# A single-core encoder block in split single precision: the rotary key's projection, the rotation, the small latent scores and the order of the first head pair are changed

## The chip, the cores and the metric

One core of a Trainium2 chip runs the whole program. Its engines are TensorE (PE: matrix products; PEld is its loading of the stationary operand), VectorE (DVE), ScalarE (ACT), GpSimd (POOL) and the DMA queues, of which this kernel uses nearly only the one that SyncE (SP) issues. Each engine carries out its own list of instructions in order; semaphores hold an instruction until what it needs is done. The metric is the device time of one execution in microseconds, smaller is better. A profiled execution gives the span from the first to the last instruction, and what each engine did in it.

## The reference, cut to what matters

272 tokens (256 real ones and 16 meta tokens) of width 2048 pass through one layer: neighbourhood attention (8 heads, "NA") and latent attention (8 heads, "MLA") side by side, an output projection, and a gated MLP. The change lies in the latent attention, where a key has 128 plain dimensions of its own head and 64 rotary ones that all heads share:

```python
def apply_rope(x, cos, sin):
    x1, x2 = x[..., :half], x[..., half:]
    return jnp.concatenate([x1 * cos - x2 * sin, x2 * cos + x1 * sin], axis=-1)
...
    q = (rmsnorm(cq, cq_g) @ w_q_up).reshape(B, L, MLA_HEADS, MLA_QK_DIM)
    kv = (rmsnorm(ckv, ckv_g) @ w_kv_up).reshape(B, L, MLA_HEADS, MLA_NOPE_DIM + MLA_V_DIM)
    k = jnp.concatenate([k_nope, jnp.broadcast_to(k_pe[:, :, None, :], (B, L, MLA_HEADS, MLA_ROPE_DIM))], axis=-1)
    q, k = rmsnorm(q, q_g), rmsnorm(k, k_g)
    q = jnp.concatenate([q[..., :MLA_NOPE_DIM], apply_rope(q[..., MLA_NOPE_DIM:], cos, sin)], axis=-1)
    k = jnp.concatenate([k[..., :MLA_NOPE_DIM], apply_rope(k[..., MLA_NOPE_DIM:], cos, sin)], axis=-1)
    s = jnp.einsum('bqhd,bkhd->bhqk', qb, k).astype(jnp.float32) * scale
```

`cq` (512 columns), `ckv` (256) and `k_pe` (64) are projections of the normed input `hn`, as are the queries, keys and values of the neighbourhood heads.

## The kernel before

**Products.** Every operand is held as a rounded part and a remainder (hi and lo). A product is then three matmuls, w_hi x_hi, w_hi x_lo and w_lo x_hi (`mm3`, lines 485 to 487, and `product3`, line 842). Tokens are the moving columns, 258 where only the queries are wanted (256 and two copied meta columns) or 272.

**Weights.** They come in pieces of up to 1024 columns (`pieces`, line 335 on). SP loads a piece into one of five `raw` buffers, ACT copies it to a `whi` buffer (four, line 450), DVE subtracts to make `wlo` (four, line 459), PE uses each 128 columns. A `raw` buffer is loaded again when its subtraction is done, a `whi`/`wlo` pair is written again when PE has used it.

**Order.** There is no scheduler on the chip for this. The program is written as threads (`Flow`, line 100), and while the kernel is built a planner with a price for each instruction decides which thread's next instruction is appended to which engine's list. What stands in the lists is then fixed; an engine that reaches an instruction too early waits, and all behind it with it.

**Stages of PE.** `attention_weights` (line 1391): projection to `cq` (64 blocks of three matmuls), to `ckv` (32), to the rotary key (16; its 64 columns stand twice in the 128 of a block), then for each of four head pairs the stages of `ORDER = "QKqkVv"`: Q, K, V are the up-projections of the latent heads (from `cq` and `ckv`), q, k, v the projections of the neighbourhood heads (from the input). Scores, softmax and products with V of one stage are laid between the projections of later ones. Then come the output projection and the MLP, which the change leaves alone.

**The steps that change.** `sum_x` (line 601) adds the squares of 16 input tiles on DVE into `sqx`; `scale_x` (line 656) sums them over partitions by a matmul with ones and makes the scales `em1` and `s1`. `compressed_kv` (line 711) normalizes `ckv`, which stage K needs. `rotary_key` (line 746) scales the projected key. `rope` (line 737) rotates: a single-precision matmul with the constant matrix `rot` swaps the halves (line 740), POOL multiplies by cos, DVE multiplies the swapped half by sin out of PSUM, POOL adds. It runs once for the key (272 columns) and once for each pair's two queries (258). `mla_rope` (line 1125) splits the rotated query into `mqr`; `mla_tile` (line 1213) uses it with both parts of the key `mkp`. `mla_small` (line 1239) makes the scores of the copied meta queries, four stationary columns `qs` for two heads: five matmuls of 272 columns for each head, ten for each pair.

Of the kernel before, what the change touches and what calls it, by code (L numbers as in the profile page):

```python
# [15 lines left out]
P = 128  # L16
# [39 lines left out]
ORDER = "QKqkVv"  # L56
# [3 lines left out]
CW = 32  # L60
KP = 2 * CW + N_META
# [14 lines left out]
CONSTS = {"ident": 0, "ones": 128, "rot": 256, "cos": 384, "sin": 384 + L}  # L76
N_CONSTS = 384 + 2 * L
# [117 lines left out]
def encoder_block(ctx: ExitStack, tc: tile.TileContext, io):  # L195
# [104 lines left out]
    class Piece:  # L300
# [6 lines left out]

        def release(self):
            fl.put(raws, self.raw)

# [36 lines left out]
    for i in range(3):  # L347
        add(io["w_in"][i])
    n_in = 3
    for pr in range(4):  # L350
        for stage in ORDER:
# [91 lines left out]
    def split_hi():  # L443
        for p in pieces:
            yield p.loaded
            p.hi = yield from one(his)
            for t, ev in zip(p.parts, p.half):
                if p is pieces[0]:
                    yield p.part[t.start]
                yield from ACT(p.hi[:, t], p.raw[:, t], AF.Copy)  # L450
                fl.set(ev)
            n_split[0] += 1

    def split_lo():
        for p in pieces:
            p.lo = yield from one(los)
            for t, ev, ready in zip(p.parts, p.half, p.ready):
                yield ev
                yield from TT(p.lo[:, t], p.raw[:, t], p.hi[:, t].bitcast(F32), ALU.subtract)
# [251 lines left out]
    def compressed_kv(pss):  # L711
        t0, t1, a, b, r = yield scr, 5
        ts = (t0, t1)
        for i, ps in enumerate(pss):
            yield from ACT(ts[i][:, :L], ps[:, :L], AF.Copy, scale=vec("g_ckv", i))
            yield from ACT((a, b)[i][:, :L], ps[:, :L], AF.Square)
            fl.put(tps, ps)
# [7 lines left out]
        for i, t in enumerate(ts):  # L725
            yield from TT(t[:, :L], t[:, :L], r[:, :L], ALU.mult)
            yield from ACT(ckv[i][0], t[:, :L], AF.Copy)
            yield from TT(ckv[i][1], t[:, :L], ckv[i][0].bitcast(F32), ALU.subtract)
            fl.put(scr, t)
        for t in (a, b, r):  # L730
            fl.put(scr, t)
        fl.set(ev_ckv)

# [3 lines left out]
    def rope(t, n, out, tmp):  # L737

        r = yield from one(sps)
        yield from MM([(r[:, :n], const("rot"), t, True, True)])  # L740
        yield from PTT(out, t, const("cos", n), ALU.mult)
        yield from TT(tmp[:, :n], r[:, :n], const("sin", n), ALU.mult)
        fl.put(sps, r)
        yield from PTT(out, out, tmp[:, :n], ALU.add)

    def rotary_key(ps):
        yield ev_s1
        t, kg, tmp = yield scr, 3
        yield from TT(t[:, :L], ps[:, :L], s1, ALU.mult)
        fl.put(acc, ps)  # L750
# [33 lines left out]
    qss = tiles(apool, 2, [P, 36], "qs", F32R)  # L784
# [104 lines left out]
    def small_queries(s):  # L889
# [3 lines left out]
        t = s.qs[:, :24].rearrange("p (l c x) -> p l c x", l=2, c=2)  # L893
        for i in range(2):
            yield "pool", 150
            nc.gpsimd.tensor_copy(t[:, i, :, 0:2], s.q[:, :, i, SEQ:NT])
        fl.set(s.ev_small)

# [145 lines left out]
    def na_small(s, pr, PT, done):  # L1044
# [7 lines left out]
        for c in range(2):  # L1052
            q = [s.qs[:, 12 * i + 4 * c : 12 * i + 4 * c + 4] for i in range(2)]
# [55 lines left out]
    mqr = Slots(tiles(apool, 1, [P, 2, NT], "mqr", F32R))  # L1109
    mk = Slots(late[6:])  # L1110
    mkp = Slots(tiles(apool, 2, [P, 2, L], "mkp", F32R))
# [13 lines left out]
    def mla_rope(s, g, t, tmp):  # L1125
# [4 lines left out]
        for c in range(2):  # L1130
            e, o = slice(64 * c, 64 * c + 64), slice(64 - 64 * c, 128 - 64 * c)
            yield from ACT(s.qr[e, c, :], t[e, :NT], AF.Copy)
            yield from TT(s.qr[o, c, :], t[e, :NT], s.qr[e, c, :].bitcast(F32), ALU.subtract)
        fl.put(scr, t)
        yield s.ev_small
        yield "pool", 150
        nc.gpsimd.tensor_copy(
            s.qs[:, 24:36].rearrange("p (c x) -> p c x", c=2)[:, :, 0:2], s.qr[:, :, SEQ:NT]
        )
# [48 lines left out]
    def mla_keys(s, c, ps):  # L1188
# [6 lines left out]
        yield from split_plain(kp[:, 0, :], kp[:, 1, :], r_)  # L1195
# [17 lines left out]
    def mla_tile(s, c, i, PT, done):  # L1213
# [9 lines left out]
            + [(S_, s.qr[:, c, q], kp[:, 0, :], False, False),  # L1223
               (S_, s.qr[:, c, q], kp[:, 1, :], False, True)]
# [14 lines left out]
    def mla_small(s, PT, done):  # L1239
# [615 lines left out]
```

## Time and profile before

| | |
|---|---|
| median of 3 runs | 1121.83 us (1121.82 to 1122.77) |
| the profiled execution | 1121.53 us |
| its span, first to last instruction | 1119.7 us |
| PE busy | 1113.9 us, 7846 matmuls |
| DVE, ACT, POOL busy | 912.5, 714.8 and 150.1 us |
| granted TensorE clock | 1.000 over the span (the level of 2.4 GHz) |

In a timeline row the first number is the start in us from the span's start, the second how long the row lasted. Matmuls overlap, and their ends are modelled; what one costs PE is the step from its start to the start of the next.

### The profile page before, as it was taken

The page shows a single profiled execution, that of the slowest core. Times are in us where ns is not written, and L with a number is a line of the kernel's source. Part 1 is how long each engine was busy: PE and PEld are TensorE (multiplying, and loading weights), DVE is VectorE, ACT ScalarE, POOL GpSimd, SP SyncE. Part 2 cuts the span into 40 slices and gives each one's busy share as a digit, 9 for nine tenths or more (in the row PEclk, how much of TensorE's full clock was granted, in tenths as well). Part 3 has the DMA queues.
Part 4 walks back from the last instruction along what each step waited for, and adds up shares of the span by engine and source line. Part 5 has one row for each costly group of instructions (what it writes and reads, how often), then busy time and mean ns, then how long its engine had stood idle before and what let it go on. Part 6 is the DMA issues. An engine that isn't in the chain of part 4 may idle for free.

```text
span 1119.7 us, 21894 instructions
## 1 busy us (share of the span) xinstructions
PE 1113.9 (99%) x7846; PEld 1043.8 (93%) x7846; DVE 912.5 (81%) x1911; ACT 714.8 (64%) x1573; POOL 150.1 (13%) x213
## 2 busy tenths in 40 slices
PE   9999999999999999999999999999999999999998
PEld 9999999999999999999999999999999988888888
DVE  8888888888877777777777777777777899999995
ACT  8787978888646655555555555555555567666763
POOL 0021112121334500010000100010001000000003
PEclk9999999999999999999999999999999999999999
DMA  9543534444655556666666666666666777677862
GB/s 352 166 160 120 168 121 143 126 144 139 226 179 180 185 169 218 219 205 204 203 224 206 202 206 222 209 197 210 213 214 206 254 268 260 238 256 266 285 241 94
DMA packets 67812, 226.68 MB, mean 202 GB/s; under 512 B 7416, under 2 KB 11000, under 8 KB 67704
## 3 DMA queue, kind: packets, MB, share of 16 engines
q1 hardware_dynamic: 67416, 225.04, 59.7%
q8 instruction: 61, 1.00, 0.4%
q14 instruction: 47, 0.39, 0.1%
q10 hardware_dynamic: 288, 0.26, 0.1%
HBM read 211.64 MB, written 13.63 MB: 201 GB/s over the span
## 4 chain that ended last, share of the span: by engine, by line
PE 94%; ACT 3%; DVE 2%; issue 1%
PE bank L1583 21%; PE bank L485 16%; PE bank L486 16%; PE bank L487 16%; PE bank L267 13%; PE bank L1584 11%; PE bank L273 2%; ACT whi L227 1%; ACT scr L227 1%; DVE scr L239 1%; DVE wlo L231 1%; ACT qraw L227 0%; PE bank L563 0%; ACT nav L227 0%; ACT bank L227 0%
## 5 line engine op out<-in xcount | busy, mean ns | idle before, releaser
L227 ACT ACTIVATE whi<-raw 128x512 fp32r<-128x512 f32 (+1 forms) x649 | 402.0, 629 | 271.2 <-PE bank L1583 115.6
L231 DVE TENSOR_TENSOR wlo<-raw,whi 128x512 fp32r<-128x512 f32 (+1 forms) x649 | 446.2, 701 | 130.8 <-ACT whi L227 127.6
L485 PE MATMUL bank<-hl,whi 128*128 128x258 f32 (+1 forms) x1232 | 356.0, 289 | 0.0
L486 PE MATMUL bank<-hl,whi 128*128 128x258 f32 (+1 forms) x1232 | 351.2, 285 | 0.0
L487 PE MATMUL bank<-hl,wlo 128*128 128x258 f32 (+1 forms) x1232 | 349.5, 284 | 0.0
L1583 PE MATMUL bank<-hl,whi 128*128 128x512 f32 x704 | 246.3, 392 | 0.0
L487 PEld LDWEIGHTS bank<-hl,wlo 128*128 128x128 f32 x1232 | 235.1, 191 | 0.1
L486 PEld LDWEIGHTS bank<-hl,whi 128*128 128x128 f32 x1232 | 234.2, 190 | 0.2
L485 PEld LDWEIGHTS bank<-hl,whi 128*128 128x128 f32 x1232 | 232.7, 189 | 1.5 <-ACT whi L227 0.3
L1584 PE MATMUL bank<-hl,wlo 128*128 128x256 f32 x704 | 197.5, 281 | 0.0
L1583 PEld LDWEIGHTS bank<-hl,whi 128*128 128x128 f32 x704 | 132.0, 188 | 28.9
L1584 PEld LDWEIGHTS bank<-hl,wlo 128*128 128x128 f32 x704 | 132.7, 188 | 0.0
L227 ACT ACTIVATE whi<-quarters 128x512 fp32r<-128x512 f32 x154 | 95.9, 631 | 54.9 <-PE bank L1583 35.7
L1583 PE MATMUL bank<-act,whi 128*128 128x512 f32 x308 | 109.9, 397 | 0.0
L255 POOL TENSOR_TENSOR mt<-mt,s 128x256 f32<-128x256 f32 x44 | 41.4, 961 | 461.6 <-ACT mt L227 461.6
L231 DVE TENSOR_TENSOR wlo<-quarters,whi 128x512 fp32r<-128x512 f32 x154 | 99.3, 691 | 3.6 <-ACT whi L227 3.2
L1584 PE MATMUL bank<-act,wlo 128*128 128x256 f32 x308 | 86.4, 280 | 0.0
L1583 PEld LDWEIGHTS bank<-act,whi 128*128 128x128 f32 x308 | 57.8, 188 | 13.8
L267 PE MATMUL bank<-whi,sin 128*128 128x512 f32 x176 | 62.5, 396 | 0.0
L1584 PEld LDWEIGHTS bank<-act,wlo 128*128 128x128 f32 x308 | 58.1, 189 | 1.6
L267 PE MATMUL bank<-whi,act 128*128 128x512 f32 x132 | 48.3, 393 | 0.0
L267 PEld LDWEIGHTS bank<-whi,sin 128*128 128x128 f32 x176 | 33.0, 188 | 7.9
(237 smaller groups left out, 1634.9 us busy)
## 6 DMA issues: line engine op xcount, KB each, us to landing
raw<-in_w_gate SPq DMA_DIRECT2D x88, 512.0 KB, 4.5
raw<-in_w_up SPq DMA_DIRECT2D x88, 512.0 KB, 4.8
raw<-in_w_in SPq DMA_DIRECT2D x54, 512.0 KB, 4.0
quarters<-in_w_down_s SPq DMA_DIRECT2D x44, 512.0 KB, 7.0
raw<-in_w_down SPq DMA_DIRECT2D x40, 512.0 KB, 5.5
raw<-in_w_out SPq DMA_DIRECT2D x32, 512.0 KB, 4.0
s_dram<-shl SPq DMA_DIRECT2D x22, 512.0 KB, 6.1
sin<-s_dram SPq DMA_DIRECT2D x22, 512.0 KB, 3.6
```

What stands on the lines that cost most here:

```text
L227: nc.scalar.activation(out, in_, f, **kw)
L231: nc.vector.tensor_tensor(out, a, b, op)
L239: nc.vector.scalar_tensor_tensor(out, a, s, b, op0, op1)
L255: nc.gpsimd.tensor_tensor(out, a, b, op)
L267: nc.tensor.matmul(o, l, r, start=start, stop=stop)
L273: nc.tensor.transpose(o, i, ident[:n, :n])
L485: nc.tensor.matmul(ps, whi, xhi, start=start, stop=False)
L486: nc.tensor.matmul(ps, whi, xlo, start=False, stop=False)
L487: nc.tensor.matmul(ps, wlo, xhi, start=False, stop=stop)
L1583: nc.tensor.matmul(ps, whi, x, start=start, stop=False)
L1584: nc.tensor.matmul(ps[:, :n], wlo, x[:, 0, :], start=False, stop=stop)
```

## The change

Five things. (1) The rotary key's weight is sent once (64 columns; `w_kpe`, one piece instead of two). Its hi and lo parts are laid side by side in the 128 stationary columns, so two matmuls for each of 16 input tiles give the key from w_hi in 64 rows and from w_lo in the other 64; ACT swaps the halves and DVE adds them. (2) `rope` no longer swaps by a matmul: four transfers from SBUF to SBUF, of 32 partitions each, are issued by SP, and DVE multiplies what they wrote by a sine table that carries the sign. (3) The small latent scores take six matmuls for each pair instead of ten: `qs` holds hi in columns 0 to 3 and lo in 32 to 35, so one pass of 36 stationary columns gives both; ACT and DVE add the two groups of rows. For this `mkp` becomes one tile with hi over lo, and `mqr` two (hi over hi, lo over zeros). (4) The first pair's order becomes `qQKkVv`. (5) `sum_x` adds on POOL (the helper `PTT`) instead of DVE, and `compressed_kv` is cut into smaller threads.

```diff
-ORDER = "QKqkVv"
+ORDERS = ("qQKkVv", "QKqkVv", "QKqkVv", "QKqkVv")
...
+    class Narrow(Piece):
+        def views(self, t):
+            out = (self.lo if t.start else self.hi).rearrange("p (k i c) -> p k i c", i=2, c=ROPE)
+            src = self.raw[:, t].rearrange("p (k c) -> p k c", c=ROPE)
+            return src, out[:, :, 0], out[:, :, 1]
...
-                yield from TT(sqx, sqx, xt[k], ALU.add)
+                yield from PTT(sqx, sqx, xt[k], ALU.add)
...
     def rope(t, n, out, tmp):
-        r = yield from one(sps)
-        yield from MM([(r[:, :n], const("rot"), t, True, True)])
+        half = ROPE // 2
+        for i in range(P // half):
+            yield "sp", 600
+            j = i ^ 1
+            swapped = Event()
+            load(tmp[i * half : (i + 1) * half, :n], t[j * half : (j + 1) * half], swapped, nc.sync)
         yield from PTT(out, t, const("cos", n), ALU.mult)
-        yield from TT(tmp[:, :n], r[:, :n], const("sin", n), ALU.mult)
-        fl.put(sps, r)
+        yield swapped
+        yield from TT(tmp[:, :n], tmp[:, :n], const("sin", n), ALU.mult)
         yield from PTT(out, out, tmp[:, :n], ALU.add)
     def rotary_key(ps):
+        t, kg, tmp = yield scr, 3
+        for c in range(2):
+            e, o = slice(64 * c, 64 * c + 64), slice(64 - 64 * c, 128 - 64 * c)
+            yield from ACT(kg[o, :L], ps[e, :L], AF.Copy)
+        yield from TT(t[:, :L], ps[:, :L], kg[:, :L], ALU.add)
+        fl.put(acc, ps)
         yield ev_s1
-        t, kg, tmp = yield scr, 3
-        yield from TT(t[:, :L], ps[:, :L], s1, ALU.mult)
-        fl.put(acc, ps)
+        yield from TT(t[:, :L], t[:, :L], s1, ALU.mult)
...
+            for i in (c, 1 - c):
+                yield from ACT(s.qr[64 * i : 64 * i + 64, c, 0, :], t[e, :NT], AF.Copy)
+                if i == c:
+                    yield from TT(
+                        s.qr[:ROPE, c, 1, :], t[e, :NT], s.qr[e, c, 0, :].bitcast(F32), ALU.subtract
+                    )
...
-        S_ = S[:4, :L]
+        S_, S2 = S[:4, :L], S[CW : CW + 4, :L]
         items = []
         for c in range(2):
-            k, kp = s.k[c], s.kp[c]
-            q = [s.qs[:, 12 * i + 4 * c : 12 * i + 4 * c + 4] for i in range(3)]
-            items += product3(S_, q[:2], (k[:, 0, :], k[:, 1, :]), c == 0, False)
-            items += [(S_, q[2], kp[:, 0, :], False, False), (S_, q[2], kp[:, 1, :], False, c == 1)]
+            k, kp, o = s.k[c], s.kp[c], QS * c
+            items += [
+                (S[:QS, :L], s.qs[:, o : o + QS], k[:, 0, :], c == 0, False),
+                (S_, s.qs[:, o : o + 4], k[:, 1, :], False, False),
+                (S[:QS, :L], s.qs[:, o + 2 * QS : o + 3 * QS], kp, False, c == 1),
+            ]
         yield from MM(items)
         sb = p[:4, :L]
-        yield from TS(sb, S_, s.rq[:4, 4:5], None, ALU.mult)
+        rq = s.rq[:4, 4:5]
+        yield from ACT(sb, S2, AF.Copy)
+        yield from TT(sb, S_, sb, ALU.add)
...
+    def project_kpe():
+        ps = yield from one(acc)
+        p = pieces[at[0]]
+        for k in range(KC):
+            yield ev_xs[k]
+            if k % 8 == 0:
+                yield p.ready[k // 8]
+            w = (p.lo if k >= 8 else p.hi)[:, k % 8 * P : (k % 8 + 1) * P]
+            yield from MM(
+                [(ps[:, :L], w, hl[k][:, i, :L], (k, i) == (0, 0), (k, i) == (KC - 1, 1))
+                 for i in range(2)]
+            )
```

Since the planner decides the lists, three places show what the edits make of them. First PE where the rotary key is projected: `hl` is the split input, `whi_88` and `wlo_92` the key's weight, `bank_72` its result. Before, the matmul of `sqx` with ones stands among the key's triples:

```order
L487 MATMUL bank_72<-hl_97,wlo_92 128x272
L267 MATMUL bank_76<-sqx,consts 128x272
L485 MATMUL bank_72<-hl_98,whi_88 128x272
L486 MATMUL bank_72<-hl_98,whi_88 128x272
L487 MATMUL bank_72<-hl_98,wlo_92 128x272
```

After, it stands ahead of them all, each input tile takes two matmuls, and behind the key comes a stage q (258 columns):

```order
L268 MATMUL bank_76<-sqx,consts 128x272
L268 MATMUL bank_72<-hl_97,whi_88 128x272 x8
L268 MATMUL bank_72<-hl_98,whi_88 128x272 x8
L268 MATMUL bank_72<-hl_99,wlo_92 128x272 x2
L268 MATMUL bank_77<-scr_145,consts 128x258
L268 MATMUL bank_72<-hl_99,wlo_92 128x272 x4
L268 MATMUL bank_76<-scr_153,consts 128x272
L268 MATMUL bank_72<-hl_100,wlo_92 128x272 x6
L274 MATMUL bank_78<-consts,few_t 4x128
L274 MATMUL bank_78<-consts,scr_145 128x128 x2
L507 MATMUL bank_73<-hl_97,whi_85 128x258
```

The `sqx` matmul moved from behind 108 of the 272-column matmuls (96 of `ckv`, 12 of the key) to behind 96. Second PE at the small latent scores of the first pair (`late` and `mkp` are the keys). Before:

```order
L267 MATMUL bank_77<-late_131,qs_174 4x272 x3
L267 MATMUL bank_77<-mkp_232,qs_174 4x272 x2
L267 MATMUL bank_77<-late_132,qs_174 4x272 x3
L267 MATMUL bank_77<-mkp_233,qs_174 4x272 x2
L267 MATMUL bank_76<-ones_r,sq8r_179 4x2 x2
```

After:

```order
L268 MATMUL bank_77<-late_131,qs_175 36x272
L268 MATMUL bank_77<-late_131,qs_175 4x272
L268 MATMUL bank_77<-mkp_233,qs_175 36x272
L268 MATMUL bank_77<-late_132,qs_175 36x272
L268 MATMUL bank_77<-late_132,qs_175 4x272
L268 MATMUL bank_77<-mkp_234,qs_175 36x272
```

Ten became six. Third the list of SP in the first pair, where the key's and the first queries' halves are swapped (`scr<-scr`). Before it held weight and bias loads only; after:

```order
L408 DMA raw_83<-in_w_in 128x1024
L408 DMA scr_150<-scr_149 32x272 x2
L408 DMA raw_84<-in_w_in 128x1024
L408 DMA scr_150<-scr_149 32x272
L408 DMA raw_80<-in_w_in 128x1024
L408 DMA scr_150<-scr_149 32x272
L408 DMA raw_81<-in_w_kv_up 128x512
L408 DMA raw_82<-in_w_in 128x1024
L408 DMA raw_83<-in_w_in 128x1024
L408 DMA scr_146<-scr_152 32x258 x4
L408 DMA raw_84<-in_w_in 128x1024
```

And DVE where it takes up what the key's four transfers wrote; the weight remainders `wlo` stand ahead of it and behind it:

```order
L232 TENSOR_TENSOR wlo_90<-raw_80,whi_86 128x512
L232 TENSOR_TENSOR wlo_91<-raw_81,whi_87 128x512
L232 TENSOR_TENSOR wlo_92<-raw_82,whi_88 128x512 x2
L232 TENSOR_TENSOR scr_150<-scr_150,consts 128x272
L232 TENSOR_TENSOR naq_225<-qraw_184,naq_225 128x258 x2
L232 TENSOR_TENSOR wlo_89<-raw_83,whi_85 128x512 x2
```

The transfers stand between loads on one queue, and DVE's sine product, which read PSUM before, now waits for the last of them.

## Rows read from the trace of the kernel before

**Rows 1.** The page's first lines: span, and busy time of each engine.
```profile
span 1119.7 us, 21894 instructions
PE 1113.9 (99%) x7846; PEld 1043.8 (93%) x7846; DVE 912.5 (81%) x1911; ACT 714.8 (64%) x1573; POOL 150.1 (13%) x213
```
**Rows 2.** Windows: stretch, its length, busy us of PE, PEld, DVE, ACT, POOL, clock, DMA.
```profile
14.00:28.00 14.00, 14.00 (x119) 14.00 (x118) 13.36 (x31) 12.82 (x29) 0.00 (x0) 1.00 0.98 375
...
320.00:600.00 280.00, 280.00 (x2068) 267.75 (x2068) 212.08 (x439) 157.60 (x297) 48.86 (x41) 1.00 0.60 199
```
**Rows 3.** Timeline of PE: the first pair's small latent scores, and what follows.
```profile
79.38 0.53 PE L267 MATMUL bank<-late,qs 128*4 128x272 f32 x3
...
80.62 0.20 PE L267 MATMUL bank<-ones_r,sq8r 128*4 128x2 f32 x2
```
**Rows 4.** Timeline of PE: the rotation matmul of pair 2, and the two rows behind it.
```profile
176.26 0.60 PE L267 MATMUL bank<-scr,consts 128*128 128x258 f32 x2
176.50 0.47 PE L485 MATMUL bank<-hl,whi 128*128 128x258 f32 x1
176.81 0.28 PE L486 MATMUL bank<-hl,whi 128*128 128x258 f32 x1
```
**Rows 5.** Timeline of PE: start of stage K, and the first pair's rotation matmul.
```profile
53.95 0.29 PE L485 MATMUL bank<-late,whi 128*128 128x272 f32 x1
54.62 0.40 PE L486 MATMUL bank<-late,whi 128*128 128x272 f32 x1 [0.38 <-DVE late L231]
...
55.73 0.62 PE L267 MATMUL bank<-scr,consts 128*128 128x272 f32 x2
56.66 0.70 PE L267 MATMUL bank<-scr,consts 128*128 128x258 f32 x2 [0.31 <-ACT scr L227]
```
**Rows 6.** Timeline of POOL: three additions of one size.
```profile
100.89 0.74 POOL L255 TENSOR_TENSOR sum_b<-sum_b,scr 128x258 f32<-128x258 f32 x1 [16.11 <-ACT scr L227]
157.62 2.43 POOL L255 TENSOR_TENSOR sum_b<-sum_b,scr 128x258 f32<-128x258 f32 x1 [12.83 <-ACT scr L227]
187.63 1.09 POOL L255 TENSOR_TENSOR sum_a<-sum_a,scr 128x258 f32<-128x258 f32 x1 [0.93 <-ACT scr L227]
```
**Rows 7.** Timeline of DVE during the second and the third of them.
```profile
157.81 1.28 DVE L231 TENSOR_TENSOR wlo<-raw,whi 128x512 fp32r<-128x512 f32 x2
...
159.47 0.91 DVE L239 SCALAR_TENSOR_TENSOR scr<-bank,rq,bias 128x272 f32<-128x272 f32 x2
...
188.00 0.73 DVE L239 SCALAR_TENSOR_TENSOR rq<-cols,rq 128x6 f32<-128x6 f32 x1
```
**Rows 8.** Groups of POOL by form: 15 additions into `kr`; busy, mean ns.
```profile
L255 POOL TENSOR_TENSOR kr<-kr,scr 128x258 f32<-128x258 f32 x15 | 24.8, 1654 | 24.7 <-ACT scr L227 24.2
```
**Rows 9.** Timeline of PE: first matmul of the `ckv` projection, and the `sqx` matmul.
```profile
28.69 0.29 PE L485 MATMUL bank<-hl,whi 128*128 128x272 f32 x1
...
42.25 0.62 PE L267 MATMUL bank<-sqx,consts 128*128 128x272 f32 x2
```
**Rows 10.** Timeline of ACT: the last three squares of the input.
```profile
35.39 1.06 ACT L227 ACTIVATE pt<-pt 128x272 f32<-128x272 f32 x3
```
**Rows 11.** DMA issues of 0 to 300 us: count, size, median us to landing.
```profile
bias<-in_na_bias SPq DMA_DIRECT2D x8, 272.0 KB, 5.9
raw<-in_w_kv_up SPq DMA_DIRECT2D x8, 256.0 KB, 2.9
```
**Rows 12.** Timeline of SP: two issues, one behind the other.
```profile
112.55 1.03 SPq L391 DMA_DIRECT2D bias<-in_na_bias  x2
```
**Rows 13.** Timeline of ACT, DVE and PE: rotated queries of pair 2, from gain to use.
```profile
175.39 0.52 ACT L227 ACTIVATE scr<-bank,gains 128x258 f32<-128x258 f32 x1
...
178.75 0.42 DVE L231 TENSOR_TENSOR scr<-bank,consts 128x258 f32<-128x258 f32 x1
...
185.70 0.42 DVE L231 TENSOR_TENSOR mqr<-scr,mqr 64x258 fp32r<-64x258 f32 x1
...
188.60 0.41 PE L267 MATMUL bank<-mkp,mqr 128*128 128x272 f32 x2
```

More of the change, by code (lines that the diff above doesn't have):

```diff
@@ L54 @@
 HW = 272
-ORDER = "QKqkVv"
+ORDERS = ("qQKkVv", "QKqkVv", "QKqkVv", "QKqkVv")
 CW = 32
+QS = CW + 4
 KP = 2 * CW + N_META
@@ L346, in encoder_block @@
     add(io["w_cq"][:, 3 * PW :])
-    for i in range(3):
+    for i in range(2):
         add(io["w_in"][i])
-    n_in = 3
+    pieces.append(Narrow(io["w_kpe"], PW))
+    n_in = 2
     for pr in range(4):
-        for stage in ORDER:
+        for stage in ORDERS[pr]:
             if stage == "Q":
@@ L446, in split_hi @@
             p.hi = yield from one(his)
+            if isinstance(p, Narrow):
+                p.lo = yield from one(los)
             for t, ev in zip(p.parts, p.half):
@@ L449, in split_hi @@
                     yield p.part[t.start]
-                yield from ACT(p.hi[:, t], p.raw[:, t], AF.Copy)
+                src, hi, _ = p.views(t)
+                yield from ACT(hi, src, AF.Copy)
                 fl.set(ev)
@@ L455, in split_lo @@
         for p in pieces:
-            p.lo = yield from one(los)
+            if not isinstance(p, Narrow):
+                p.lo = yield from one(los)
             for t, ev, ready in zip(p.parts, p.half, p.ready):
                 yield ev
-                yield from TT(p.lo[:, t], p.raw[:, t], p.hi[:, t].bitcast(F32), ALU.subtract)
+                src, hi, lo = p.views(t)
+                yield from TT(lo, src, hi.bitcast(F32), ALU.subtract)
                 fl.set(ready)
@@ L714, in compressed_kv @@
         for i, ps in enumerate(pss):
-            yield from ACT(ts[i][:, :L], ps[:, :L], AF.Copy, scale=vec("g_ckv", i))
             yield from ACT((a, b)[i][:, :L], ps[:, :L], AF.Square)
-            fl.put(tps, ps)
+        fl.spawn(latent_gained(pss, ts))
         yield from TT(a[:, :L], a[:, :L], b[:, :L], ALU.add)
@@ L725, in compressed_kv @@
         for i, t in enumerate(ts):
[L726 to L729, printed above, removed]
+            fl.spawn(latent_scaled(i, t, r))
+        for i in range(2):
+            yield ev_ckvs[i]
         for t in (a, b, r):
@@ L732, in compressed_kv, with latent_gained, latent_scaled @@
         fl.set(ev_ckv)
+    ev_ckvs = [Event(), Event()]
+    def latent_gained(pss, ts):
+        for i, ps in enumerate(pss):
+            yield from ACT(ts[i][:, :L], ps[:, :L], AF.Copy, scale=vec("g_ckv", i))
+            fl.put(tps, ps)
+    def latent_scaled(i, t, r):
+        yield from TT(t[:, :L], t[:, :L], r[:, :L], ALU.mult)
+        yield from ACT(ckv[i][0], t[:, :L], AF.Copy)
+        yield from TT(ckv[i][1], t[:, :L], ckv[i][0].bitcast(F32), ALU.subtract)
+        fl.put(scr, t)
+        fl.set(ev_ckvs[i])
     kr = apool.tile([P, L], F32, name="kr")
@@ L1052, in na_small @@
         for c in range(2):
-            q = [s.qs[:, 12 * i + 4 * c : 12 * i + 4 * c + 4] for i in range(2)]
+            q = [s.qs[:, QS * c + CW * i : QS * c + CW * i + 4] for i in range(2)]
             items += product3(
@@ L1130, in mla_rope @@
         for c in range(2):
-            e, o = slice(64 * c, 64 * c + 64), slice(64 - 64 * c, 128 - 64 * c)
-            yield from ACT(s.qr[e, c, :], t[e, :NT], AF.Copy)
-            yield from TT(s.qr[o, c, :], t[e, :NT], s.qr[e, c, :].bitcast(F32), ALU.subtract)
+            e = slice(64 * c, 64 * c + 64)
+            for i in (c, 1 - c):
[4 more added lines that the diff above has]
+                    )
         fl.put(scr, t)
         yield s.ev_small
[L1136 to L1139, printed above, removed]
+        for i in range(2):
+            yield "pool", 150
+            nc.gpsimd.tensor_copy(few(s.qs, 2 * QS, i), s.qr[:, :, i, SEQ:NT])
         fl.set(s.ev_qr)
@@ L1389, in project @@
         return pss
+    def project_kpe():
[10 more added lines that the diff above has]
+            )
+        for _ in range(8):
+            used()
+        return ps
     def attention_weights():
@@ L1442, in attention_weights @@
             started = False
-            for stage in ORDER:
+            for stage in ORDERS[pr]:
                 if stage in "QKV":
@@ L1743, in _layout @@
     for pr in range(4):
-        for stage in ORDER:
+        for stage in ORDERS[pr]:
             if stage not in "qkv":
```

48 lines of the change are left out of this document (25 added, 23 removed).

## Prediction, made before the changed kernel was run

> **What bounds the kernel now.** I read the page's first lines first: PE is busy 1113.9 of 1119.7 us, DVE 912.5 [rows 1]. A busy PE need not be at its pace, so the windows come next: in the MLP PE is busy every microsecond (280.00 of 280) while DVE has 68 us to spare, and the clock column says 1.00, the 2.4 GHz level [rows 2]. Then the timeline of PE, for the step from one matmul's start to the next. Ten matmuls of 272 columns, with only four stationary columns, take from 79.38 to 80.62, so 0.124 us each [rows 3]; 108 full ones take from 28.69 to 42.25, 0.1256 each [rows 9]. So a matmul costs PE its moving columns, nothing for the stationary ones, and PE's list is nearly the whole time. A matmul taken out of it is a gain at once; what is put on another engine costs nothing until PE has to wait for it. PE's waits are few and short; the two longest behind the start are at the head of stage K and at the first pair's rotation [rows 5].
>
> **What goes from PE.** The key's projection: 16 blocks of three matmuls become 16 of two, 16 x 0.124 = 2.0 us. The small scores: four pairs, ten matmuls to six, 16 x 0.124 = 2.0 us; that the stationary side grows from 4 to 36 columns costs nothing, since 128 columns run at the same step [rows 3, 9]. The rotation: five matmuls in single precision. One takes 0.24 us to the next start, and the matmul behind it then takes 0.31 where about 0.12 is usual [rows 4], so 0.24 + 0.19 = 0.43, five times: 2.15 us. Sum 6.15 us, all on the path, since PE ran without a gap around them.
>
> **What waits go.** At the head of stage K a step of 0.67 (53.95 to 54.62) stands where 0.124 is usual; PE waits for the last part of `ckv` [rows 5]. With stage q of the first pair put ahead, 96 matmuls of about 0.12, 11.5 us, lie between: the wait, 0.55 us, is covered. The first rotation begins 0.93 after the matmul ahead of it, 0.68 more than the 0.24 to 0.25 of a normal one, for ACT's scaled query [rows 5]. It goes with the matmul: 0.7. Together 1.25, and with the 6.15 above 7.4 us.
>
> **What comes, off PE.** ACT gets two half swaps, eight copies for `mqr`, four for the small scores, and loses two weight splits; DVE gets four small additions and loses two splits and 15 additions. Neither is full over the attention stage (the whole-run shares are 64% and 81% [rows 1]), and I cost these at nothing, under PE's matmuls; if that cover were gone, a split would come late by about one such step, some 0.4 us. Two edits have a price that the trace does not show directly.
>
> First, the 15 additions on POOL. One of 258 columns takes 0.74 us when DVE is quiet, and 2.43 or 1.09 when it is not [rows 6]. During the 2.43 DVE ran subtractions with both inputs in SBUF (157.81 to 159.09), and POOL ended 0.6 after DVE began to read a PSUM bank at 159.47; during the 1.09 a DVE step of only six columns took 0.73 [rows 7]. So each holds the other up. Into `kr`, 15 additions took 1.65 us on average [rows 8]. The last squares are ready at 36.45 [rows 10], and PE will ask for the sum behind 96 instead of 108 matmuls, at 28.69 + 96 x 0.1256 = 40.75 [rows 9]. If four additions are then still open (my assumption), the sum stands at 39.4 with 0.74 each, at 43.05 with 1.65, at 46.2 with 2.43. DVE has most of its gaps there, as PE sets its pace by then, so I take a value near the lower end, with no wait for the sum, and 0.5 us for the start of the program, where DVE is busy 13.36 of 14 us [rows 2] and a POOL addition in a gap can delay a split that PE is about to use. Ends: 0, and 5.5 (46.2 - 40.75).
>
> The Trainium skill ("SBUF — State Buffer", Who interferes with whom) says that a DVE instruction with two SBUF inputs and a GpSimd instruction that reads SBUF shut each other out for a whole instruction. By that rule the edit moves work onto the very port it is meant to relieve. The trace agrees on the mechanism (2.43 against 0.74 us); how often it strikes in the first 40 us no row shows, since POOL does nothing there before.
>
> Second, the rotation by transfers: 20 of them, four in a set, on SP's queue. Two issues take 1.03 us [rows 12], so four take 2.06. No row shows a transfer from SBUF to SBUF; loads of 256 and 272 KB land after 2.9 and 5.9 us [rows 11]. Each of these carries 33 KB, so I take 2.9 as the nearer row; below it is possible, above it too when a load stands ahead. In pair 2 before, DVE began its sine product 2.84 us after ACT had the query (175.91 to 178.75), and the second half of the split query was ready at 186.12 for a use at 188.60: 2.48 us of slack [rows 13]. With transfers the first distance is 2.06 + 2.9 = 4.96, which is 2.1 later: covered, 0.4 left. On SP the next weight loads stand behind a set and start up to 2 us later; behind DVE's sine product stand weight remainders. A `raw` buffer is loaded anew five pieces, or about 15 us of PE, ahead of its next use (24 matmuls of 0.125 for each piece), against a landing of 2.9 to 5.9, so the loads have room. I take 0.4 us for small waits of these chains, ends 0 and 10.5 (below).
>
> **Sum.** 7.4 - 0.5 - 0.4 = 6.5 us less than the profiled execution: 1121.53 - 6.5 = 1115.0. The median of the runs is 0.3 above that execution, so 1115.3. What is late next is again PE: stages behind start 6.5 us earlier as a whole.
>
> **Rivals.**
> *A, the sum on POOL is late.* PE stands at the `sqx` matmul, and `em1`, the `ckv` scale and the first pair hang on it. Against it: DVE's gaps from 33 us on. For it: rows 6 to 8. At the 1.65 of `kr` the wait is 43.05 - 40.75 = 2.3 us, 1117.6; at 2.43 it is 5.5, 1120.8, no change that can be measured. It begins to cost at 1.07 us for an addition.
> *B, slower: the transfers land late, and the queries' rotation gates the scores.* If a set lands after 5.9 us, the distance is 2.06 + 5.9 = 7.96, 5.1 later than before against a slack of 2.48: PE stands 2.6 us at each pair's first score, four pairs 10.5 us, 1125.8. It costs from a landing of 3.3 us, and turns the change slower than before from 4.9. For it: the sets share rings with 512 KB loads. Against it: a transfer of 33 KB is an eighth of the smaller row, and the first set's loads are spaced over a stage.
> *C, more waits go.* The new order also takes the short waits of pairs 1 to 3, some 0.2 to 0.3 us each as the 0.31 in rows 5: up to 2 us, 1113.3.
> *D, the gain is not kept.* If the MLP were held by weights and not by PE, it would end when it does now: 1121.8. The 280.00 of 280 in rows 2 speaks against it.
>
> **How the numbers follow.** Forecast (1113.4 to 1117.2) 0.60, C below it 0.08, A between 1117.2 and 1119.6 0.17, A or B near no change 0.08, D 0.03, B slower 0.04. The range from 1113.0 to 1119.4 takes in the forecast, most of A and a part of C, 0.8 or a little more. Runs of this kernel can tell 0.2%, 2.2 us, from no change: faster than 1119.6 is 0.60 + 0.08 + 0.17 = 0.85, within 2.2 us 0.11, slower 0.04.
>
> **What would show it.** In the profile after: 37 matmuls less on PE and PE busy down by about 6; the small scores at six steps of 0.124; no single-precision matmul at a pair's start; no wait at the head of stage K. POOL's 15 additions show whether they take 0.74 or over 1.07 each, and the step ahead of the `sqx` matmul whether PE waits. The landing of a set and the idle time of DVE ahead of its sine product, and of PE ahead of the first `mkp,mqr`, decide B. I am wrong if PE's new waits add up to more than about 4 us, or if the step of a 36-column pass is longer than 0.124.

## The result, and the profile after

The changed kernel takes 1115.35 us (median; 1115.20 to 1115.78), the kernel before on the same chip 1122.07 (1121.82 to 1122.77). The ratio is 0.994, with an interval of 0.9923 to 0.9957: 6.7 us less. The forecast was 1115.3. The profiled execution of after took 1115.78 us, 5.75 less than that of before, where the sum had said 6.5.

The page's first lines of after, which answer to [rows 1]:

```profile
span 1114.0 us, 21868 instructions
PE 1107.7 (99%) x7804; PEld 1038.7 (93%) x7804; DVE 913.2 (82%) x1900; ACT 717.2 (64%) x1585; POOL 164.6 (15%) x232
```

PE is busy 6.2 us less, and the span is 5.7 us shorter. There are 42 matmuls less and not 37, since the trace has two records for each of the five in single precision. POOL has 14.5 us more, and DVE lost its 15 additions but is busy 0.7 us more than before. The windows of [rows 2], of after (stretch, length, busy us and instructions of PE, PEld, DVE, ACT, POOL, then clock, DMA share, GB/s):

```profile
14.00:28.00 14.00, 13.97 (x116) 13.77 (x115) 13.53 (x26) 12.97 (x30) 5.50 (x6) 1.00 0.98 368
320.00:600.00 280.00, 280.00 (x2055) 267.19 (x2055) 211.83 (x440) 158.32 (x298) 46.76 (x39) 1.00 0.61 199
```

The MLP is as it was, PE busy in all of its 280 us, so nothing that was gained ahead of it is given back there. At the start DVE is as full as before (13.53 of 14 us against 13.36), with 5.50 us of POOL beside it.

PE's timeline of after (start, length, engine, line, operation, count): stage K's head, for the first part of [rows 5], and the first pair's small scores, for [rows 3]:

```profile
64.44 0.29 PE L507 MATMUL bank<-late,whi 128*128 128x272 f32 x1
64.57 0.29 PE L508 MATMUL bank<-late,whi 128*128 128x272 f32 x1
...
95.16 0.41 PE L268 MATMUL bank<-late,qs 128*36 128x272 f32 x2
95.41 0.29 PE L268 MATMUL bank<-mkp,qs 128*36 128x272 f32 x1
95.53 0.41 PE L268 MATMUL bank<-late,qs 128*36 128x272 f32 x2
```

Three matmuls go from 95.16 to 95.53, 0.123 each, as those with four stationary columns did before. Two of the three have 36 stationary columns and one has four (a merged row shows the shape of its first). Stage K's first step is 0.13, where 0.67 stood. The waits of PE that the trace names in after (for whom; us in total, times, longest) begin with the one at the program's start that the kernel before has too:

```profile
PE bank L585 <- DVE em L583: 1.2, 1, 1.2
PE bank L268 <- POOL sq8r L256: 0.5, 2, 0.3
PE bank L508 <- DVE hl L240: 0.3, 1, 0.3
PE bank L268 <- DVE wlo L232: 0.2, 1, 0.2
PE bank L507 <- ACT whi L228: 0.2, 1, 0.2
PE bank L268 <- POOL sqx L256: 0.2, 1, 0.2
```

For the experiments I split the time from PE's first projection matmul to the first of the output projection (whose operand is `ob`) by what PE worked on, as the sum of the steps from each row of its timeline to the next. A wait is counted to the row ahead of it. From there on the kernels run alike to about 0.5 us. Pairs are counted from 1 here, so the prediction's pair 2 is pair 3. "Fp32" are the single-precision matmuls (sums over `sqx` and `scr`, and the rotation), "ones" the sums with `ones_r`.

| us | sum | projections | small scores | fp32 | transposes | ones | scores, products with V |
|---|---|---|---|---|---|---|---|
| before | 282.19 | 223.85 | 4.99 | 3.58 | 14.50 | 5.21 | 30.06 |
| after | 275.90 | 222.03 | 3.07 | 1.39 | 14.70 | 5.68 | 29.03 |

Projections give 1.8, small scores 1.9, single precision 2.2 us, together 5.9. The last column holds 250 matmuls in both kernels. Of its 1.0 us, 0.55 are two steps of the kernel before, in pairs 3 and 4, that take 0.41 and 0.39 us where 0.13 is usual. The one in pair 3 lies between the second matmul of the last line of [rows 13], at 188.72, and this one:

```profile
189.14 0.40 PE L267 MATMUL bank<-late,mq 128*128 128x272 f32 x1
```

### The profile page after: what moved, and what is told of

Its sections match the earlier page's. It is cut to its first block, busy times and chain, and to the rows that moved or that the text cites. A ratio compares the mean times of both kernels' runs of the same rounds, so it can differ in the third digit from the quotient of the medians.

```text
span 1114.0 us, 21868 instructions
## 1 busy us (share of the span) xinstructions
PE 1107.7 (99%) x7804; PEld 1038.7 (93%) x7804; DVE 913.2 (82%) x1900; ACT 717.2 (64%) x1585; POOL 164.6 (15%) x232
## 4 chain that ended last, share of the span: by engine, by line
PE 91%; ACT 3%; DVE 3%; issue 1%; POOL 1%; DMA 0%; ACTq 0%; DVEq 0%; POOLq 0%
PE bank L1658 21%; PE bank L508 15%; PE bank L507 15%; PE bank L509 15%; PE bank L268 13%; PE bank L1659 11%; PE bank L274 1%; ACT whi L228 1%; DVE wlo L232 1%; DVE scr L240 1%; ACT scr L228 1%; POOL sqx L256 0%; DMA raw<-in_w_cq 0%; DVE cols L248 0%; ACT mqr L228 0%
## 5 line engine op out<-in xcount | busy, mean ns | idle before, releaser
L507 PE MATMUL bank<-hl,whi 128*128 128x258 f32 (+1 forms) x1216 | 350.6, 288 | 0.3 <-ACT whi L228 0.2
L508 PE MATMUL bank<-hl,whi 128*128 128x258 f32 (+1 forms) x1216 | 346.5, 285 | 0.3 <-DVE hl L240 0.3
L509 PE MATMUL bank<-hl,wlo 128*128 128x258 f32 (+1 forms) x1216 | 344.6, 283 | 0.0
L508 PEld LDWEIGHTS bank<-hl,whi 128*128 128x128 f32 x1216 | 230.9, 190 | 0.8 <-DVE hl L240 0.7
L507 PEld LDWEIGHTS bank<-hl,whi 128*128 128x128 f32 x1216 | 229.4, 189 | 1.8 <-ACT whi L228 0.5
L1658 PEld LDWEIGHTS bank<-hl,whi 128*128 128x128 f32 x704 | 132.0, 188 | 28.9
L240 DVE SCALAR_TENSOR_TENSOR mt<-mt,vecs,mt 128x256 f32<-128x256 f32 x88 | 40.4, 480 | 0.0
```

The source lines that it names most:

```text
L240: nc.vector.scalar_tensor_tensor(out, a, s, b, op0, op1)
L507: nc.tensor.matmul(ps, whi, xhi, start=start, stop=False)
L508: nc.tensor.matmul(ps, whi, xlo, start=False, stop=False)
L509: nc.tensor.matmul(ps, wlo, xhi, start=False, stop=stop)
L1658: nc.tensor.matmul(ps, whi, x, start=start, stop=False)
```

## Experiments

Timed beside the kernels below, the kernel before took 1121.8 to 1122.0. "Over after" means over 1115.35.

### One part undone, all lists laid anew

The first four were meant to price the parts one by one.

**Order.** The first pair's order goes back.

```diff
-ORDERS = ("qQKkVv", "QKqkVv", "QKqkVv", "QKqkVv")
+ORDERS = ("QKqkVv", "QKqkVv", "QKqkVv", "QKqkVv")
```

> The changed kernel with the first pair's stages in the old order (QKqkVv); all else stays. My theory (PE's list is the time; the order only takes waits away): stage K of the first pair again stands close behind the ckv projection, its wait of about 0.55 us comes back, and the first pair's rotation by transfers has less cover, up to 1 us more; 1115.9 to 1116.9 against 1115.35 of the changed kernel. Rival (the new lists, not the matmuls left out, are the gain): 3 us or more slower, 1118.4 and above.

Measured: 1119.30 us, 3.95 over after.

**Sum.** `sum_x` goes back to DVE.

```diff
-                yield from PTT(sqx, sqx, xt[k], ALU.add)
+                yield from TT(sqx, sqx, xt[k], ALU.add)
```

> The changed kernel with the 15 additions of squares on DVE again. My theory: they are off PE's path on either engine but for the 0.32 us that PE waits for the sum in the changed kernel; 1114.9 to 1115.9. Rival A (POOL and DVE shut each other out, and this costs PE): the early waits of the changed kernel go, 0.5 to 1 us faster, 1114.4 to 1114.8. Opposite rival (DVE needs the room): 1 us or more slower, 1116.4 and above.

Measured: 1119.92 us, 4.6 over after. The largest step over the usual lies nowhere near the sum, but at the `nak,ones_r` matmul of the first pair (timeline of PE in this kernel):

```profile
84.00 0.29 PE L509 MATMUL bank<-hl,wlo 128*128 128x272 f32 x1
85.08 0.52 PE L268 MATMUL bank<-nak,ones_r 128*128 128x272 f32 x2 [0.80 <-ACT p L228]
```

A step of 1.08 stands where 0.13 is usual, and the trace puts 0.80 of it down to an activation of ACT, the exponential of another softmax.

**Rotation.** `rope` swaps by a matmul again, with the old tables.

```diff
...
-            load(tmp[i * half : (i + 1) * half, :n], t[j * half : (j + 1) * half], swapped, nc.sync)
...
+        yield from MM([(r[:, :n], const("rot"), t, True, True)])
...
```

> The changed kernel with the five rotations by a matmul with the constant matrix again, no transfers. My theory: five single-precision matmuls at 0.43 us come back to PE, 2.15 us, and up to 0.7 for their wait: 1117.5 to 1118.2. Rival (the transfers cost in waits what they save): within 0.7 us of the changed kernel, 1114.7 to 1116.0.

Measured: 1120.86 us, 5.5 over after.

**Key.** The weight comes twice again, three matmuls for an input tile.

```diff
...
-        ps = yield from project_kpe()
+        (ps,) = yield from project(1, L)
...
```

> The changed kernel with the rotary key's weight twice in its block and three matmuls for each of 16 input tiles (two pieces of weight, four splits). My theory: 16 matmuls at 0.125 us come back, 2.0 us: 1117.0 to 1117.9. Rival (this stretch is held by splits and the sum of squares, not by PE): the 16 matmuls fill waits, 0.7 us or less slower, up to 1116.0.

Measured: 1121.84 us, 6.5 over after.

A fifth followed when these were known:

**Small scores.** Ten matmuls for a pair, in the new layout of `qs`.

```diff
...
-                (S[:QS, :L], s.qs[:, o : o + QS], k[:, 0, :], c == 0, False),
-                (S_, s.qs[:, o : o + 4], k[:, 1, :], False, False),
-                (S[:QS, :L], s.qs[:, o + 2 * QS : o + 3 * QS], kp, False, c == 1),
...
+            items += product3(S_, q[:2], (k[:, 0, :], k[:, 1, :]), c == 0, False)
+            items += [(S_, q[2], kp, False, False), (S_, q[3], kp, False, c == 1)]
...
```

> The small latent scores of the four pairs go back to ten matmuls, 16 more in all. Price alone: 16 x 0.124 = 2.0 us, 1117.3 (1117.0 to 1117.8), if the parts add. If the four undone parts before this one cost 4.0 to 6.5 us because every edit makes the planner lay all lists anew, and not by their own price, this one too costs more than its price: 1118.0 to 1121.5, with the same 0.124 us steps, and the rest as steps of TensorE that run 0.2 to 1 us over the usual in places that have nothing to do with the small scores.

Measured: 1121.67 us, 6.3 over after.

What follows. The first four expectations were all too low, by 2.4 us or more; for the order and for the sum it was the rival, the larger loss, that came. The fifth counted on such a loss, and its range ended 0.2 us below the time. The five losses add up to 26.8 us, where the whole change gained 6.7. So the parts cannot be priced in this way: every edit, however small, makes the planner lay new lists for all engines, and something in them costs about the same each time. That it is the lists is only argued so far; the runs further down test it. Less the price of the matmuls that come back (0 for the sum, 2.15, 2.0 and 2.0 for the next three), 4.6, 3.4, 4.5 and 4.3 us are left.

### The same lists with matmuls added, or with an engine exchanged

To price a part without new lists, the planner must not know of it.

**32 matmuls twice.**

```diff
-    def MM(items):
+    def MM(items, again=0):
         yield "pe", sum(cost(l, r) for _, l, r, _, _ in items)
-        for o, l, r, start, stop in items:
+        for j, (o, l, r, start, stop) in enumerate(items):
             nc.tensor.matmul(o, l, r, start=start, stop=stop)
+            if j < again:
+                nc.tensor.matmul(o, l, r, start=False, stop=False)
...
```

with `again` 1 at each of the key's 16 tiles and 4 at each pair's small scores.

> The lists stay as they are, and 32 matmuls of 272 columns run a second time that the planner is not told of: one more for each of the key's 16 input tiles, and four more in each pair's small scores (so the key and these scores are not the reference's). Theory: on TensorE's path each costs its step of 0.124 us and nothing else, 32 x 0.124 = 4.0 us, 1119.3 (1118.9 to 1119.9); so undoing these two edits with the lists kept costs 4.0, and what the undone key costs beyond its 2.0 us is the lists. Rival, that a matmul more in these places is worth about 3 steps (what undoing the key gave: 6.5 us for 16): 1125 and above. Other rival, that waits of TensorE take part of it up: under 1118.5.

Measured: 1119.49 us, 4.1 over after, for 32 matmuls: 0.129 us each. Projections rose by 1.92 us and small scores by 1.97, and no other column of the table by more than 0.01 (the scores' fell by 0.1). PE's step is the whole price, at both places.

**The sum on DVE, booked on POOL.**

```diff
-                yield from PTT(sqx, sqx, xt[k], ALU.add)
+                yield "pool", 90 + 2.7 * NT
+                nc.vector.tensor_tensor(sqx, sqx, xt[k], ALU.add)
```

> The 15 additions of the input's squares run on VectorE, but the planner still books them on GpSimd, so every other list stays as it is (undoing this part with new lists cost 4.6 us). Theory of the lists: the additions themselves are worth about nothing either way, since TensorE waits 0.3 us for the sum with GpSimd and VectorE has room before 41 us: 1114.9 to 1116.2. Rival, that taking 15 additions off VectorE while it prepares the input is what gains: they hold up the splits, 1117.5 to 1120.

Measured: 1115.22 us, level with after (1114.99 to 1115.37). The additions in after, by form, and below them those of this kernel (count; busy, mean ns):

```profile
L256 POOL TENSOR_TENSOR sqx<-sqx,pt 128x272 f32<-128x272 f32 x15 | 15.2, 1011 | 24.3 <-ACT pt L228 18.4 <-issue 4.4 <-POOL sqx L256 0.7
```
```profile
L630 DVE TENSOR_TENSOR sqx<-sqx,pt 128x272 f32<-128x272 f32 x15 | 6.5, 436 | 0.3
```

So moving the sum to POOL is worth nothing by itself; what undoing it cost, 4.6 us, was the lists. The move did not even empty DVE. Its windows around the sum (columns as above) and its subtractions in them, by form, first in after, then in this kernel:

```profile
14.00:42.00 28.00, 27.81 (x224) 27.35 (x222) 26.80 (x44) 24.23 (x58) 15.16 (x15) 1.00 0.83 295
L232 DVE TENSOR_TENSOR wlo<-raw,whi 128x512 fp32r<-128x512 f32 x21 | 17.1, 846 | 0.4 <-ACT whi L228 0.2
```
```profile
14.00:42.00 28.00, 28.00 (x229) 27.92 (x229) 26.91 (x62) 24.26 (x58) 0.00 (x0) 1.00 0.80 292
L232 DVE TENSOR_TENSOR wlo<-raw,whi 128x512 fp32r<-128x512 f32 x22 | 14.6, 685 | 0.3 <-PE bank L509 0.3
```

With 6.5 us of additions DVE is busy 26.91 of 28 us, and without them 26.80: beside POOL's additions a subtraction takes 0.85 us instead of 0.69.

### The lists alone

**One number of the planner**, its assumed delay from another engine to PE, in both kernels: no instruction changes, only the order.

```diff
-    TO_PE, FROM_PE, OTHER = 700.0, 200.0, 140.0
+    TO_PE, FROM_PE, OTHER = 720.0, 200.0, 140.0
```

For the changed kernel with 720:

> The changed kernel with one number of the planner changed, its delay to TensorE 720 instead of 700 ns: the same instructions, in another order from the first pair on. Theory that the lists are worth several us by themselves: 1 to 4 us slower than with 700, 1116.4 to 1119.4, with TensorE as busy as before (1107.7 us) and the difference in waits. Rival, that the undone parts cost what they cost by themselves: 1115.0 to 1115.8 for this one.

For the kernel before with 720, the changed one with 640 and the one before with 640:

> The kernel before with the planner's delay to TensorE 720 instead of 700 ns; the same instructions in other lists. Theory that the gain belongs to the instructions and that the lists of each kernel were tuned at 700: this one is 1 to 6 us slower than before, 1123 to 1128, and the changed kernel at 720 (1119.2) stands some 4 to 8 us below it. Rival, that the change's gain is a lucky list and nothing more: this one 1119 to 1120.5, level with the changed kernel at 720.

> The changed kernel with the delay at 640. Same instructions, lists that differ at nearly 8,000 places on TensorE. Theory of the lists: 1116.5 to 1121. Rival, that the list with 720 was one bad one and others do as well as 700: 1114.8 to 1116.

> The kernel before with the delay at 640. By the theory 4 to 8 us above the changed kernel at 640; by the rival of the lucky list level with it, within 1.5 us.

| us | before | changed | difference |
|---|---|---|---|
| 640 | 1122.03 | 1118.85 | 3.2 |
| 700 | 1121.80 | 1115.35 | 6.5 |
| 720 | 1121.74 | 1119.18 | 2.6 |

The changed kernel loses 3.5 and 3.8 us with other lists, as the theory said. The kernel before doesn't move at all, against the theory, which had its lists tuned as well. Both named sizes failed there: neither 1123 to 1128 for the kernel before at 720, nor a level pair as by the lucky list. The truth lies between: 2.6 to 3.2 us of the gain stay with the other two lists, and 3.3 to 3.9 hang on the one laid with 700.

Where they go, by the steps of PE:

| us | sum | projections | small scores | fp32 | transposes | ones | scores, products with V |
|---|---|---|---|---|---|---|---|
| after | 275.90 | 222.03 | 3.07 | 1.39 | 14.70 | 5.68 | 29.03 |
| after, 640 | 279.18 | 222.47 | 2.99 | 1.37 | 15.15 | 7.37 | 29.83 |
| after, 720 | 280.01 | 223.43 | 3.03 | 1.55 | 15.38 | 6.91 | 29.71 |

The removed matmuls stay removed in all three. Waits come back in nearly every kind of work, with 640 most of all at the sums with `ones_r` (1.7 us), with 720 in the projections (1.4) and at these sums (1.2). PE's busy time goes with them, to 1110.0 us with 640 and 1110.2 with 720, though 1107.7 was expected for 720: the modelled ends (0.29 us for a step of 0.125) count short waits as work. One of the waits can be followed. PE's `ones_r,sq8r` rows of pairs 3 and 4, first in after, then with 640:

```profile
180.82 0.24 PE L268 MATMUL bank<-ones_r,sq8r 128*4 128x2 f32 x4
...
239.14 0.24 PE L268 MATMUL bank<-ones_r,sq8r 128*4 128x2 f32 x4
```
```profile
182.52 0.17 PE L268 MATMUL bank<-ones_r,sq8r 128*4 128x2 f32 x1
183.18 0.22 PE L268 MATMUL bank<-ones_r,sq8r 128*4 128x2 f32 x3 [0.49 <-POOL sq8r L256]
...
241.91 0.17 PE L268 MATMUL bank<-ones_r,sq8r 128*4 128x2 f32 x1
242.56 0.22 PE L268 MATMUL bank<-ones_r,sq8r 128*4 128x2 f32 x3 [0.49 <-POOL sq8r L256]
```

The first matmul needs the rounded half, made by DVE, the next the remainder, made by POOL. POOL's and DVE's rows at that place, first POOL and DVE in after, then POOL and DVE with 640:

```profile
180.22 0.20 POOL L256 TENSOR_TENSOR sq8r<-sq,sq8r 128x8 fp32r<-128x8 f32 x1
180.22 0.74 DVE L232 TENSOR_TENSOR wlo<-raw,whi 128x512 fp32r<-128x512 f32 x1
```
```profile
182.55 0.58 POOL L256 TENSOR_TENSOR sq8r<-sq,sq8r 128x8 fp32r<-128x8 f32 x1 [0.71 <-DVE sq8r L244]
```
```profile
182.38 0.68 DVE L232 TENSOR_TENSOR wlo<-raw,whi 128x512 fp32r<-128x512 f32 x1
```

The same eight columns take 0.20 us or 0.58. In after DVE's next subtraction begins at the same time as POOL's work, at 180.22, and it is DVE's that is a little longer, 0.74. With 640 DVE had started a subtraction with two inputs in SBUF 0.17 us earlier, and POOL ended at 183.13, just behind DVE's 183.06. The Trainium skill ("SBUF — State Buffer", Who interferes with whom) says that these two shut each other out; the rows agree, at a price of 0.38 us here. It happens in both pairs, twice 0.49 of PE's wait. In the steps of PE that is 0.6 us a pair, 1.2 of the 3.3 us. The conflict itself accounts for no more than 0.38 a pair. For the rest, PE comes to these matmuls earlier, 0.05 us behind DVE's rounding (182.31 and 0.16 long) where it came 0.7 behind it in after. And the kernel before, laid with 640, has a wait at the same place, 0.6 us in all, and is no slower:

```profile
PE bank L267 <- POOL sq8r L255: 0.6, 2, 0.3
```

### Late transfers

**Each set is sent twice more ahead of itself,** by eight transfers that the planner doesn't know of; the lists are those of after.

```diff
         for i in range(P // half):
             yield "sp", 600
             j = i ^ 1
             swapped = Event()
+            if i == 0:
+                for _ in range(2):
+                    for m in range(P // half):
+                        nc.sync.dma_start(
+                            tmp[m * half : (m + 1) * half, :n], t[(m ^ 1) * half : ((m ^ 1) + 1) * half]
+                        )
```

> Ahead of each set of rotation transfers the same data are sent twice more, by eight transfers that the planner does not know of; the lists stay as they are, and a set is there 8 x 0.59 = 4.7 us later (some 7 to 8 us after its first issue). By the rival that late transfers decide (slower than before from a landing at 4.9 us), each pair's first work waits some 4 us: 1128 to 1135. By the theory that TensorE has other work in its list there, but in a fixed order that cannot be changed while it runs, the wait shows in full as soon as the sine product is late: some 3 us x 4 pairs, 1124 to 1130. If the landing has a margin of over 5 us nothing shows: 1115.2 to 1116.5.

Measured: 1131.68 us (1130.13 to 1133.03), 16.3 over after and 1.0087 of before (1.0072 to 1.0102). That is in the range of the first rival and above that of the theory, but the waits are not some 4 us in each pair. First pair, pair 3 and pair 4 on PE's timeline, pair 3's sine product on DVE's, and DVE's waits for the sets (total, times, longest), all of this kernel:

```profile
65.28 0.29 PE L509 MATMUL bank<-late,wlo 128*128 128x272 f32 x1
69.66 0.60 PE L507 MATMUL bank<-late,whi 128*128 128x272 f32 x1 [4.08 <-ACT qraw L228]
70.05 0.43 PE L508 MATMUL bank<-late,whi 128*128 128x272 f32 x1
70.27 0.43 PE L509 MATMUL bank<-late,wlo 128*128 128x272 f32 x1
...
189.86 0.28 PE L509 MATMUL bank<-hl,wlo 128*128 128x258 f32 x1
192.68 0.17 PE L268 MATMUL bank<-ones_r,sq8r 128*4 128x2 f32 x1 [2.54 <-DVE sq8r L244]
...
254.18 0.17 PE L268 MATMUL bank<-ones_r,sq8r 128*4 128x2 f32 x1 [0.98 <-DVE sq8r L244]
```
```profile
192.12 0.43 DVE L232 TENSOR_TENSOR scr<-scr,consts 128x258 f32<-128x258 f32 x1 [3.83 <-DMA scr<-scr]
```
```profile
DVE scr L232 <- DMA scr<-scr: 16.0, 5, 7.5
```

In the first pair DVE stands 7.5 us for the key's set and PE 4.1 behind it. The sine product of pair 3 comes 19.32 us behind the start of its stage Q (172.80) instead of 15.42, 3.9 later, and PE waits 2.7 more; in pair 4 it is 2.33 later and PE waits 1.14. Both leave a slack of 1.2 us in the changed kernel. But the long steps of PE in this kernel, six of 0.5 to 4.3 us over the usual that after does not have, add up to 10.1 us and not to 16. The steps behind the first wait are 0.22, not 0.13. The windows of this kernel (columns as above) say why:

```profile
64.00:70.00 6.00, 1.92 (x12) 1.62 (x12) 1.60 (x3) 1.68 (x8) 1.02 (x2) 0.86 0.72 224
70.00:76.00 6.00, 5.13 (x24) 4.72 (x23) 4.11 (x14) 4.86 (x18) 2.61 (x6) 0.50 0.37 111
82.00:90.00 8.00, 7.97 (x68) 7.77 (x67) 7.29 (x19) 6.58 (x19) 1.47 (x4) 1.00 0.73 249
195.00:198.00 3.00, 3.00 (x16) 3.00 (x15) 2.61 (x9) 2.60 (x8) 0.00 (x0) 0.50 0.85 322
254.00:258.00 4.00, 3.33 (x29) 3.25 (x30) 4.00 (x13) 2.26 (x8) 1.47 (x2) 1.00 0.97 307
```

Behind PE's wait the granted clock is 0.50, the level of 1.2 GHz, and only later 1.00 again. It falls a second time behind the 2.54 us of pair 3, and not behind the 0.98 of pair 4 (the last window). Over the span it is 0.994, so 0.006 x 1129 = 6.8 us were withheld, a part of it while PE waited anyway. By the steps, the stretch of the table above takes 291.65 us instead of 275.90; less the 10.1 of waits, 5.7 us are left, most of them in these two places. A long wait is paid for twice.

## Why the prediction came out right, step by step

**What goes from PE: right.** Small scores lost 1.9 us where 2.0 was said, and the kernel with 32 matmuls twice gives 0.129 for each against the 0.124 used, at the key and at the small scores. The projections' 1.8 is no check of the key's 2.0. Before, that column also held the slow matmuls behind four rotations, some 0.19 us too long each, and stage K's wait of 0.55; they are gone too, so 3.3 us should have left it, and 1.5 came back in it as other long steps. Single precision lost 2.2, with the first rotation's wait in it, and the five matmuls themselves are gone. PE is busy 6.2 us less, near the 6.15 of the sum, but with other lists the same matmuls show 1110.0 and 1110.2, so that agreement proves little.

**What waits go: right in place, not in balance.** Both waits of [rows 5] are gone. But the steps over the usual from 0 to 290 us add up to about 5 us in after as before: what the two gave, 1.25, came back as other waits of 0.2 to 0.5, where the sum allowed 0.9. The difference, 0.3 us, is about half of what separates 6.5 from the profiled 5.75.

**The sum on POOL: right by a hair.** The break-even was 1.07 us for an addition, and the mean is 1.011. Row by row (PE, then POOL, of after):

```profile
41.05 0.29 PE L509 MATMUL bank<-hl,wlo 128*128 128x272 f32 x1
41.50 0.72 PE L268 MATMUL bank<-sqx,consts 128*128 128x272 f32 x2 [0.17 <-POOL sqx L256]
```
```profile
35.04 6.41 POOL L256 TENSOR_TENSOR sqx<-sqx,pt 128x272 f32<-128x272 f32 x6 [3.16 <-issue]
```

The last six additions take 6.41 us and end at 41.45, not at 39.4; my 0.74 for each was too low, and six stood at the end where I had assumed four. PE asked at 41.18 and waits 0.3 us. The reason that I gave for a low value was wrong too. DVE had no gaps there, neither before (the window, columns as above) nor in after, where its subtractions fill the time of these additions:

```profile
33.00:41.00 8.00, 8.00 (x66) 8.00 (x66) 7.79 (x16) 5.67 (x15) 0.00 (x0) 1.00 0.50 157
```
```profile
36.42 4.40 DVE L232 TENSOR_TENSOR wlo<-raw,whi 128x512 fp32r<-128x512 f32 x4
```

That the sum came late by no more than 0.3 us was luck in part. Here the rule of the Trainium skill that the prediction weighed ("SBUF — State Buffer", Who interferes with whom) can be seen at work: 1.01 us on average beside a full DVE against 0.74 beside a quiet one (258 columns), and these four subtractions take 1.10 us each, not 0.68. The rows show less than a whole instruction of waiting, as far as POOL's rough spans tell: an addition and a subtraction side by side start anew every 1.1 us, and 0.74 and 0.68 end to end would be 1.4. Rival A's mechanism is there at that size. The 0.5 us that I set down for the start of the program is about this size, but not at this place.

**The transfers: right.** Issues and landings of a set in after (count, size, median us to landing; then one set's four issues on SP, and the first use):

```profile
scr<-scr SPq DMA_DIRECT2D x16, 32.2 KB, 2.4
...
scr<-scr SPq DMA_DIRECT2D x4, 34.0 KB, 4.4
```
```profile
67.09 2.41 SPq L408 DMA_DIRECT2D scr<-scr  x4
```
```profile
61.46 0.44 DVE L232 TENSOR_TENSOR scr<-scr,consts 128x272 f32<-128x272 f32 x1 [0.82 <-DMA scr<-scr]
```

The queries' sets land after 2.4 us where I took 2.9, and four issues take 2.41 where I took 2.06; the two misses cancel. DVE waits once, for the key's set, 0.82 us, and PE does not notice. Rival B did not come, with 1.2 us of slack where the prediction had 0.4. The late sets show that its mechanism is real. They also show that its price was too low: it counted PE's waits alone, and not the clock behind them.

**Rivals C and D: no.** Some waits of later pairs did go: PE's steps of 0.34 to 0.54 us at 133.74, 186.10, 188.72, 245.82 and 248.48 of the kernel before, 1.4 us over the usual, have no like in after, where from 150 us to the output projection no step is that long. Other waits came in ahead of 135 us, so no gain of C's was left. The MLP did not take the gain back.

**What the prediction did not see.** It summed the parts as if the lists were given. They are not: with two other delays the same instructions take 1118.85 and 1119.18, and a forecast of 6.5 for those kernels would have been 3.5 to 3.9 us off, at the edge of the range. That the allowance of 0.9 us for new waits held is a property of the lists laid with 700, which the trace of before could not show. In that sense the number was right partly by luck. The undone kernels point the same way. Undoing the sum, the rotation, the key or the small scores left a loss of 3.4 to 4.6 us beyond the matmuls, and 640 and 720 lose 3.5 and 3.8: six other lists stand about alike, and the one laid with 700 alone is better. As far as these runs go that list is the exception, and with another one the edits would have gained some 3 us and not 6.5. Why the kernel before is indifferent to its lists and the changed one is not stays open: the wait at `sq8r` is some 1.2 us of one of the two losses, at most 0.8 of that by the conflict, and the others are spread over waits of 0.1 to 0.8 us in all columns of the table. Three delays are too few to settle it.

## What to carry to other kernels

Where PE never stands, price a removed matmul by its step: for 32 of them that held within 5% here. Do not take PE's busy time for the check, since short waits hide in it. Where a planner lays the order, do not price the parts by undoing them one at a time; keep the lists and slip the work in or out behind the planner's back, and vary one number of the planner to see how much the lists alone are worth before calling a gain the edit's own. For a kernel that leans on one list, that number belongs among the things to tune again after every edit.

## What the hardware showed beyond expectation

- A wait of PE of 4.1 us was followed by a granted clock of 0.50 in all of the 6 us from 70.00 on, the level of 1.2 GHz, with steps of 0.22 us instead of 0.13, and the clock was back at 1.00 by 82.00. A wait of 2.54 us was followed by 0.50 from 195 to 198 us, and one of 0.98 us by none. Of the 16.3 us that late transfers cost, some 5.7 are the clock.
- Eight columns on POOL take 0.20 us or 0.58, by whether DVE has begun a two-input subtraction in SBUF just before. An addition of 272 columns beside a busy DVE took 1.01 us on average, and four of DVE's subtractions beside them 1.10 each instead of 0.68.
- Four transfers of 32 KB within SBUF land after 2.4 us each (median), the issue of one taking 0.59 us of SP's queue. Those of the key's set, issued while weights were loading, landed after 4.4.
- 6.5 us of additions on DVE and 15.2 us of them on POOL cost the same to a tenth of a microsecond. Taking them off DVE left it as busy as before (26.80 of 28 us against 26.91), since its own instructions became longer beside POOL's.
